# RMS norms of a transformer kernel: the squares of the last feature blocks go to TensorE as further operands of the sum over partitions

## The chip, the cores and the metric

The kernel runs on one core of one Trainium2 chip. The metric is the device time of one execution in microseconds (us), given as the median of three runs. Five parts of the core matter here: PE (TensorE; its weight loads are listed apart as PEld), DVE (VectorE), ACT (ScalarE), POOL (GpSimd), and the DMA queue that SP (SyncE) issues.

## What is computed

Two blocks, one after the other, on 256 tokens of 1024 features. The first has two attention branches and a mixture of experts; the second has two layers, each with a half feed-forward, a mixing step and another half feed-forward, and it works on a second stream of 256 context tokens beside the first. Between the steps stand RMS norms, and this change is about those:

```python
def _rmsnorm(x, g):
    x32 = x.astype(jnp.float32)
    y = x32 * lax.rsqrt(jnp.mean(x32 * x32, axis=-1, keepdims=True) + EPS)
    return (y * g.astype(jnp.float32)).astype(x.dtype)

def _half_ffn(h, g, shift, scale, gate, w_up, w_down):
    return h + 0.5 * gate * _swiglu(_modulate(_rmsnorm(h, g), shift, scale), w_up, w_down)
```

For one token a norm needs the sum of the squares of its 1024 features.

## The kernel before

The hidden state `h` lies with features on the 128 partitions: eight blocks of 128 features (index `d`, 0 to 7), each with 512 columns, of which 256 are the tokens of stream `v` = 0 and 256 those of stream 1. The sum over a token's features is therefore a sum over eight blocks and then over partitions.

A weight matrix comes by DMA as fp32, is split into a high and a low part (`split_w`, ACT L228 and mostly DVE L237, sometimes POOL L235), and each product is three matmuls, lines L250, L251 and L252. This stream of matmuls is nearly all that PE does. Tiles named `pab` are the first product of a feed-forward, `pd` its second, `pj` an input projection and `po` the output of mixing.

A norm is made of these steps:

- As blocks of `h` are finished (DVE L700, `residual`), ACT squares them: two blocks at a time in `square` (L345), one at a time in `square1` (L356). The squares land in a scratch tile `sq`, and scratch tiles rotate through seven buffers.
- POOL adds the squares to a running sum `sqa` of 128 x 256 (L349 for the first pair; L351 adds the halves of a later pair, and L352 adds that to `sqa`; L357 adds a single block).
- The last pair (`i == last`) or the last block (`d == 7`) is added by DVE in place of POOL. In the output of a feed-forward, blocks 6 and 7 come singly: 6 is added by POOL and 7 by DVE. In mixing and in the first block all four pairs are added as pairs, the last one by DVE with two additions.
- `rstd` (L319) sums over partitions: for each half of 128 tokens one matmul with the squares as its weights and a single column of ones as the moving operand, into the tile `ss`. Then DVE makes `nv` (L325) and the reciprocal root (`rsqrt`, L292 to L303).
- `spread` (L315) turns the result into a row for all partitions (tile `rb`), and `apply` makes the next step's operands `xH` and `xL` from it (DVE L333, ACT L338, DVE L339).

There are twelve such norms in an execution. Seven follow a feed-forward and use `square1`; five use `square` alone: one of the context tokens, one ahead of the experts, two after the mixing of layer 0, and one after the mixing of layer 1. The last of the five is used late: its factor is applied to the product of the next feed-forward and not to its input (`late_norm`, L372). After the last feed-forward, `finish` (L1739) scales `h`, transposes it (`op`, L1749) and writes it out.

The order in which instructions stand on an engine comes from a scheduler that works with its own cost estimates; generators with constants such as `NORM_LAG` say only after how many steps of the main work a norm's parts are recorded. On an engine, instructions run in the order in which they stand.

Of the kernel before, what the change touches and what calls it, by code (L numbers as in the profile page):

```python
# [12 lines left out]
ALU = mybir.AluOpType  # L13
# [5 lines left out]
S = 256  # L19
# [151 lines left out]
class Builder:  # L171
# [147 lines left out]
    def rstd(self, sq):  # L319
        nc = self.nc  # L320
        ss = self.nps("ss")
        for t in range(2):
            nc.tensor.matmul(ss[:, t:t + 1], sq[0][:, t * 128:(t + 1) * 128], self.ones[:, 0:1], start=True, stop=True)
        m = self.small([128, 2], "nv")
        nc.vector.tensor_scalar(m, ss[:, :2], 1.0 / D, EPS, ALU.mult, ALU.add)  # L325
        return self.rsqrt(m, 2, "nr")
# [14 lines left out]
    def square(self, v, i, sq, last=3):  # L341
        nc = self.nc
        t = self.s512("sq")
        hs = self.h[:, 2 * i:2 * i + 2, v * S:(v + 1) * S]
        nc.scalar.activation(t.rearrange("p (j t) -> p j t", j=2), hs, AF.Square)  # L345
        e = nc.vector if i == last else nc.gpsimd
        if not sq:
            sq.append(self.scr.tile([128, S], F32, tag="sqa", name="sqa", bufs=2))
            e.tensor_tensor(sq[0], t[:, :S], t[:, S:], ALU.add)  # L349
        else:  # L350
            e.tensor_tensor(t[:, :S], t[:, :S], t[:, S:], ALU.add)  # L351
            e.tensor_tensor(sq[0], sq[0], t[:, :S], ALU.add)  # L352

    def square1(self, v, j, sq, e):
        t = self.s512("sq")[:, :S]
        self.nc.scalar.activation(t, self.h[:, j, v * S:(v + 1) * S], AF.Square)  # L356
        e.tensor_tensor(sq[0], sq[0], t, ALU.add)  # L357

    def normed(self, l, n, v, sq):
        for _ in range(NORM_LAG[v][0 if n < 2 else 2]):  # L360
# [228 lines left out]
    def ffn(self, l, n, up, dn, vs, side, pace, after):  # L589
        nc = self.nc  # L590
        self.raw_n, self.raws = 0, 7
        half = lambda v: slice(v * S, (v + 1) * S)
        with ExitStack() as st:
# [9 lines left out]
            for pi, nf in enumerate(PARTS):  # L603
# [6 lines left out]
                for c in range(nf // 2):  # L610
# [4 lines left out]
                    for i in range(2):  # L615
# [20 lines left out]
                        for z in range(0, len(todo), 2):  # L636
                            pa, pb = todo[z][1][:, full], todo[z + 1][1][:, full]
                            if late:
                                p = pabs.pop(0)
                                ab = self.small([128, 2], "ab")  # L640
                                s = self.s512("fs").rearrange("p (a t) -> p a t", a=2)
# [4 lines left out]
                                t = self.s512("ft")[:, full]  # L646
                                nc.vector.scalar_tensor_tensor(t, s[:, 1], ab[:, 1:2], s[:, 0], ALU.add, ALU.mult)
                            else:
                                s = self.s512("fs")[:, full]
                                nc.scalar.activation(s, pa, AF.Silu)  # L650
                                t = self.s512("ft")[:, full]
# [9 lines left out]
                if pi < len(PARTS) - 1:  # L661
                    for dc in range(4):
                        v = self.rows(dn, f0 * 128, nf, dc * 256, 256)
                        for i in range(2):
                            w = self.split_w(v[:, :, i * 128:(i + 1) * 128], off_dn)
                            p = self.mm("pd")
                            self.gemm(p[:, full], w, lambda f: hid[f])
                            for v2 in range(N // S):
                                self.residual(p[:, half(v2)], 2 * dc + i, l, n, v2)
                        for _ in range(pace[1] if N == full_n else 1):  # L670
                            next(side, None)
                else:
                    ws = [self.split_w(self.rows(dn, f0 * 128, nf, dc * 256, 256), OFF_256) for dc in range(4)]
                    for v in sorted(vs):
                        sq = []
                        for d in range(KD):
                            cs = slice(d % 2 * 128, d % 2 * 128 + 128)
                            w = [z[:, :, cs] for z in ws[d // 2]]
                            p = self.mm("pd")[:, :S]
                            self.gemm(p, w, lambda f: (hid[f][0][:, half(v)], hid[f][1][:, half(v)]))  # L680
                            self.residual(p, d, l, n, v)
                            next(side, None)
                            self.advance()
                            if d >= 6:
                                self.square1(v, d, sq, nc.vector if d == 7 else nc.gpsimd)
                            elif d % 2:
                                self.square(v, d // 2, sq)
                        for _ in side:
                            pass
                        self.settle()  # L690
                        if after is not None:
                            self.pending = self.normed(*after, v, sq)
                        else:
                            self.sq = sq
# [1107 lines left out]
```

## Time and profile before

| | |
|---|---|
| median of 3 runs | 2226.15 us (2225.15 to 2231.33) |
| the profiled execution | 2228.05 us |
| its span in the trace | 2226.3 us |
| PE busy, share of the span | 2157.4 us, 97% |
| PEld busy | 1779.4 us, 80% |
| DVE busy | 1437.8 us, 65% |
| ACT busy | 816.7 us, 37% |
| POOL busy | 170.9 us, 8% |
| granted TensorE clock, mean | 0.993 |

The profiled execution is 1.75 us longer than its span, and 1.9 us above the median. Matmuls overlap each other and their weight loads, so the duration of one is not its price: the price is the step from one start to the next.

### The profile page before, as it was taken

How to read it: one execution, taken by the hardware profiler on the slowest of the kernel's cores; microseconds unless marked ns; L12 is line 12 of the kernel's file. 1: busy time of each engine (PE TensorE's matmuls, PEld its weight loads, DVE VectorE, ACT ScalarE, POOL GpSimd, SP SyncE). 2: the span in 40 equal slices, each digit the busy share in tenths (PEclk: the TensorE clock that was granted, in tenths of full speed). 3: DMA queues.
4: the chain of work that ended last, by engine and by line, in shares of the span. 5: the costliest groups of instructions: out<-in, count | busy, mean ns of one | idle time of the engine just before them, and what ended most of it. 6: DMA issues, size and time to landing. Idle time of an engine off the chain costs nothing.

```text
span 2226.3 us, 32470 instructions
## 1 busy us (share of the span) xinstructions
PE 2157.4 (97%) x13295; PEld 1779.4 (80%) x13295; DVE 1437.8 (65%) x2520; ACT 816.7 (37%) x1256; POOL 170.9 (8%) x200
## 2 busy tenths in 40 slices
PE   8999999997999999989999999999999999999998
PEld 7789975543688888977888777788878888889998
DVE  5656852321489787766678777638974346877666
ACT  4564431200233322447542222234222223575443
POOL 0100100000000000340120000000000003312000
PEclk9999999999999999999999999999999999999999
DMA  8673869998956654320236555343553222317551
GB/s 259 230 242 129 274 226 353 361 387 350 336 169 212 226 187 151 88 66 29 97 123 200 182 189 181 127 132 112 192 189 100 90 66 73 105 34 246 176 174 48
DMA packets 285461, 395.91 MB, mean 178 GB/s; under 512 B 18156, under 2 KB 220540, under 8 KB 285180
## 3 DMA queue, kind: packets, MB, share of 16 engines
q1 hardware_dynamic: 284288, 392.33, 52.2%
q8 instruction: 106, 1.74, 0.3%
q0 software_dynamic: 576, 1.18, 0.2%
q14 instruction: 47, 0.39, 0.0%
q10 hardware_dynamic: 444, 0.27, 0.0%
HBM read 392.71 MB, written 1.05 MB: 177 GB/s over the span
## 4 chain that ended last, share of the span: by engine, by line
PE 68%; DVE 5%; ACT 1%; POOL 1%; issue 1%; DMA 0%; ACTq 0%; POOLq 0%; DVEq 0%
PE pab L250 12%; PE pab L251 12%; PE pab L252 12%; PE pd L250 6%; PE pd L251 6%; PE pd L252 6%; PE pj L250 1%; PE pj L252 1%; PE pj L251 1%; PE egu L1164 1%; PE aT L1654 1%; PE as L1625 1%; DVE w L237 1%; PE ada_ps L533 1%; PE ao L1671 1%; DVE xL L339 1%
## 5 line engine op out<-in xcount | busy, mean ns | idle before, releaser
L228 ACT ACTIVATE w<-raw 128x1024 fp32r<-128x1024 f32 (+2 forms) x432 | 425.8, 991 | 667.4 <-PE pd L252 240.5
L237 DVE TENSOR_TENSOR w<-raw,w 128x1024 fp32r<-128x1024 f32 (+2 forms) x422 | 481.5, 1151 | 185.8 <-ACT w L228 184.0
L251 PE MATMUL pab<-xL,w 128*128 128x512 f32 (+2 forms) x1600 | 545.7, 342 | 2.6 <-DVE xL L339 1.6
L250 PE MATMUL pab<-xH,w 128*128 128x512 f32 (+2 forms) x1600 | 546.0, 342 | 0.1
L252 PE MATMUL pab<-xH,w 128*128 128x512 f32 (+2 forms) x1600 | 544.1, 340 | 0.0
L250 PEld LDWEIGHTS pab<-xH,w 128*128 128x128 f32 x1600 | 301.4, 189 | 48.9 <-issue 8.2
L251 PEld LDWEIGHTS pab<-xL,w 128*128 128x128 f32 x1600 | 301.8, 189 | 42.3 <-issue 4.1
L252 PEld LDWEIGHTS pab<-xH,w 128*128 128x128 f32 x1600 | 301.7, 189 | 37.9 <-issue 4.1
L551 DVE SCALAR_TENSOR_TENSOR acc<-raw,sT,acc 128x512 f32<-128x512 f32 x420 | 285.0, 748 | 0.0
L250 PE MATMUL pd<-hH,w 128*128 128x512 f32 (+1 forms) x800 | 265.4, 334 | 0.5 <-ACT hH L241 0.3
L251 PE MATMUL pd<-hL,w 128*128 128x512 f32 (+1 forms) x800 | 265.0, 332 | 0.0
L252 PE MATMUL pd<-hH,w 128*128 128x512 f32 (+1 forms) x800 | 264.5, 332 | 0.0
L250 PE MATMUL pj<-xH,w 128*128 128x256 f32 (+1 forms) x816 | 247.8, 305 | 12.0 <-DVE qra L1553 5.2
L251 PE MATMUL pj<-xL,w 128*128 128x256 f32 (+1 forms) x816 | 242.8, 298 | 1.5 <-DVE xL L339 0.5
L252 PE MATMUL pj<-xH,w 128*128 128x256 f32 (+1 forms) x816 | 241.9, 297 | 0.5 <-DVE w L237 0.5
L250 PEld LDWEIGHTS pj<-xH,w 128*128 128x128 f32 x816 | 154.7, 190 | 26.5 <-DVE qra L1553 6.0
L700 DVE SCALAR_TENSOR_TENSOR h<-pd,gmod,h 128x256 f32<-128x256 f32 x224 | 101.0, 480 | 101.3 <-PE pd L252 101.2
L250 PEld LDWEIGHTS pd<-hH,w 128*128 128x128 f32 x800 | 149.8, 188 | 20.4 <-ACT fs L650 3.4
L252 PEld LDWEIGHTS pd<-hH,w 128*128 128x128 f32 x800 | 149.9, 188 | 16.7 <-issue 1.7
L251 PEld LDWEIGHTS pd<-hL,w 128*128 128x128 f32 x800 | 150.8, 188 | 15.5 <-DVE hL L242 0.3
L251 PEld LDWEIGHTS pj<-xL,w 128*128 128x128 f32 x816 | 155.1, 190 | 7.2 <-DVE xL L339 2.2
L252 PEld LDWEIGHTS pj<-xH,w 128*128 128x128 f32 x816 | 154.8, 190 | 5.5 <-DVE w L237 0.8
(388 smaller groups left out, 2456.3 us busy)
## 6 DMA issues: line engine op xcount, KB each, us to landing
raw<-ffn_up SPq DMA_DIRECT2D x94, 1024.0 KB, 5.3
raw<-w_ada SPq DMA_DIRECT2D x72, 1024.0 KB, 5.3
raw<-ffn_down SPq DMA_DIRECT2D x52, 768.0 KB, 4.7
raw<-w_in SPq DMA_DIRECT2D x32, 1024.0 KB, 5.5
raw<-w_exp_gate SPq DMA_DIRECT2D x32, 1024.0 KB, 9.7
raw<-w_exp_up SPq DMA_DIRECT2D x32, 1024.0 KB, 10.0
raw<-w_exp_down SPq DMA_DIRECT2D x32, 1024.0 KB, 8.8
raw<-w_gate SPq DMA_DIRECT2D x8, 1024.0 KB, 5.7
```

Of the source, the lines that this page charges most:

```text
L228: self.nc.scalar.activation(wh, v, AF.Copy)
L237: self.nc.vector.tensor_tensor(wl, v, wh.bitcast(F32), ALU.subtract)
L250: mm(o, wH[:, k, :], aH, start=(first and k == 0), stop=False)
L251: mm(o, wH[:, k, :], aL, start=False, stop=False)
L252: mm(o, wL[:, k, :], aH, start=False, stop=(last and k == n - 1))
L339: nc.vector.scalar_tensor_tensor(lo, t, B(j), hi.bitcast(F32), ALU.add, ALU.subtract)
L533: mm(ps[g * 32:(g + 1) * 32, :], self.unit[:, 31 - r:63 - r], acc[v], start=(u < 2), stop=(u > 3))
L551: ins = V.scalar_tensor_tensor(acc[v], w[:, g, :], s, acc[v], ALU.mult, ALU.add)
L700: self.nc.vector.scalar_tensor_tensor(hs, p, self.gmod[:, l, n, d, v:v + 1], hs, ALU.mult, ALU.add)
L1164: mm(pr[a * 64:a * 64 + 64, m, :], xg[p // 2][:, q * 2 + kk, es[a] % 4 * 64:es[a] % 4 * 64 + 64], w[:, a, kk * 512:(kk + 1) * 512], start= ...
L1625: mm(o[:, c], qs, x[i][:, c], start=(i == 0 and not (near and c.start == 0)), stop=(i == 1))
L1654: nc.tensor.transpose(T[:, j * 128:(j + 1) * 128], e[:, a, j * 128:(j + 1) * 128], self.ident)
```

## The change

`square` and `square1` no longer add the last squares to the running sum. They put the tiles of squares into a list behind it, and `rstd` runs one matmul for each operand of the list, all accumulating into the same column of `ss`. In every norm the list then has three operands: `sqa` with six blocks, and the last two blocks.

```diff
@@ rstd
         for t in range(2):
-            nc.tensor.matmul(ss[:, t:t + 1], sq[0][:, t * 128:(t + 1) * 128], self.ones[:, 0:1], start=True, stop=True)
+            for i, s in enumerate(sq):
+                nc.tensor.matmul(ss[:, t:t + 1], s[:, t * 128:(t + 1) * 128], self.ones[:, 0:1],
+                                 start=(i == 0), stop=(i == len(sq) - 1))
@@ square
-        e = nc.vector if i == last else nc.gpsimd
-        if not sq:
+        e = nc.gpsimd
+        if i == last:
+            sq.extend((t[:, :S], t[:, S:]))
+        elif not sq:
             sq.append(self.scr.tile([128, S], F32, tag="sqa", name="sqa", bufs=2))
             e.tensor_tensor(sq[0], t[:, :S], t[:, S:], ALU.add)
         else:
             e.tensor_tensor(t[:, :S], t[:, :S], t[:, S:], ALU.add)
             e.tensor_tensor(sq[0], sq[0], t[:, :S], ALU.add)
 
-    def square1(self, v, j, sq, e):
+    def square1(self, v, j, sq):
         t = self.s512("sq")[:, :S]
         self.nc.scalar.activation(t, self.h[:, j, v * S:(v + 1) * S], AF.Square)
-        e.tensor_tensor(sq[0], sq[0], t, ALU.add)
+        sq.append(t)
@@ ffn
-                                self.square1(v, d, sq, nc.vector if d == 7 else nc.gpsimd)
+                                self.square1(v, d, sq)
```

The instructions also change places, since the scheduler orders them anew. On PE, at the end of the first feed-forward of layer 0 (first of its two norms), the difference reads (- before, + now):

```order
 L251 MATMUL pd<-hL,w 128x256
 L252 MATMUL pd<-hH,w 128x256
-L323 MATMUL ss<-sqc,sqa 128x1 x2
+L324 MATMUL ss<-sqc,sqa 128x1
+L324 MATMUL ss<-sqc,sq 128x1 x2
+L324 MATMUL ss<-sqc,sqa 128x1
+L324 MATMUL ss<-sqc,sq 128x1 x2
 L250 MATMUL pd<-hH,w 128x256
 L251 MATMUL pd<-hL,w 128x256
```

Two matmuls became six at the same place in the stream. So it is in five of the norms: the first one, and the first norm of each of the four pairs.

On PE in the first part of the last feed-forward (the late norm), two pieces. Before, the two matmuls stood here:

```order
L252 MATMUL pab<-xH,w 128x258
L323 MATMUL ss<-sqc,sqa 128x1 x2
L250 MATMUL pab<-xH,w 128x258
L251 MATMUL pab<-xL,w 128x258
L252 MATMUL pab<-xH,w 128x258
```

Now the matmul on `sqa` stands 34 matmuls further ahead, between products that were there before, and the other five stand 20 matmuls ahead of the old place:

```order
 L250 MATMUL pab<-xH,w 128x258 x2
 L251 MATMUL pab<-xL,w 128x258
+L324 MATMUL ss<-sqc,sqa 128x1
 L252 MATMUL pab<-xH,w 128x258
 L250 MATMUL pab<-xH,w 128x258
```

The second norm of each of the four pairs is moved ahead in the same way, by smaller distances.

On PE at the end of the program, the matmuls on squares now stand before and after nine of the sixteen transposes of the output:

```order
 L251 MATMUL pd<-hL,w 128x256
 L252 MATMUL pd<-hH,w 128x256
-L323 MATMUL ss<-sqc,sqa 128x1 x2
-L1749 MATMUL op<-sqc,h 128x128 x16
-L1798 UNCONDITIONAL_BRANCH
+L324 MATMUL ss<-sqc,sqa 128x1
+L324 MATMUL ss<-sqc,sq 128x1
+L1753 MATMUL op<-sqc,h 128x128 x9
+L324 MATMUL ss<-sqc,sq 128x1
+L324 MATMUL ss<-sqc,sqa 128x1
+L324 MATMUL ss<-sqc,sq 128x1 x2
+L1753 MATMUL op<-sqc,h 128x128 x7
```

At that place one addition of POOL and one of DVE (L357) are gone. Around the experts' start the order of the first products and of the routing is changed in several rows, on PE, DVE and ACT.

## Rows read from the trace of the kernel before

**Rows 1.** The page: busy time of the engines (share of the span, instructions).

```profile
PE 2157.4 (97%) x13295; PEld 1779.4 (80%) x13295; DVE 1437.8 (65%) x2520; ACT 816.7 (37%) x1256; POOL 170.9 (8%) x200
```

**Rows 2.** Instructions by tile, `sqa`: count, duration in ns (min/median/max), first and last start.

```profile
L323 PE MATMUL ss<-sqc,sqa x48: 164/250/271, 259.2 to 2218.0; 128*128 128x1 f32 x48
...
L357 POOL TENSOR_TENSOR sqa<-sqa,sq x7: 730/744/823, 907.0 to 2215.9; 128x256 f32<-128x256 f32 x7
L357 DVE TENSOR_TENSOR sqa<-sqa,sq x7: 414/426/427, 908.0 to 2217.2; 128x256 f32<-128x256 f32 x7
L352 DVE TENSOR_TENSOR sqa<-sqa,sq x5: 419/421/426, 246.2 to 2027.7; 128x256 f32<-128x256 f32 x5
```

**Rows 3.** Timeline at the first norm: start, duration, engine, [idle before <- releaser].

```profile
259.07 0.53 PEld L323 LDWEIGHTS ss<-sqc,sqa 128*128 128x128 f32 x4
...
259.51 0.19 PEld L250 LDWEIGHTS pj<-xH,w 128*128 128x128 f32 x1
```

**Rows 4.** Timeline at the norm that follows the experts, matmuls of two columns.

```profile
594.59 0.98 PEld L1213 LDWEIGHTS sums<-fin,sq 128*128 128x128 f32 x8
...
595.49 0.19 PEld L251 LDWEIGHTS pab<-xL,w 128*128 128x128 f32 x1
```

**Rows 5.** Timeline at the last norm.

```profile
2216.64 0.42 ACT L356 ACTIVATE sq<-h 128x256 f32<-128x256 f32 x1 [0.87 <-DVE h L700]
2217.16 0.43 DVE L357 TENSOR_TENSOR sqa<-sqa,sq 128x256 f32<-128x256 f32 x1 [0.61 <-ACT sq L356]
...
2217.64 0.61 PE L323 MATMUL ss<-sqc,sqa 128*128 128x1 f32 x4 [3.97 <-DVE sqa L357]
...
2218.28 0.16 DVE L325 TENSOR_SCALAR nv<-ss 128x2 f32<-128x2 f32 x1 [0.43 <-PE ss L323]
```

**Rows 6.** Timeline at the norm ahead of the experts.

```profile
281.54 0.61 PE L323 MATMUL ss<-sqc,sqa 128*128 128x1 f32 x4 [0.81 <-DVE sqa L352]
```

**Rows 7.** The waits of PE, whole span: us in total, times, longest.

```profile
PE rb L315 <- DVE nr_y L303: 1.9, 4, 0.6
...
PE pab L251 <- DVE xL L339: 1.6, 5, 0.6
...
PE pab L251 <- DVE xL L1496: 0.7, 3, 0.3
...
PE pj L251 <- DVE xL L339: 0.5, 2, 0.3
```

**Rows 8.** Timeline: transposes of the second norms after the first feed-forward, both layers.

```profile
929.22 0.45 PE L315 MATMUL rb<-sqc,nr_y 128*128 128x128 f32 x2 [0.50 <-DVE nr_y L303]
...
1892.07 0.45 PE L315 MATMUL rb<-sqc,nr_y 128*128 128x128 f32 x2 [0.56 <-DVE nr_y L303]
```

**Rows 9.** Timeline at the late norm.

```profile
2024.59 0.28 PE L252 MATMUL pab<-xH,w 128*128 128x258 f32 x1
...
2024.64 1.76 DVE L237 TENSOR_TENSOR w<-raw,w 128x1024 fp32r<-128x1024 f32 x1
...
2025.39 1.60 POOL L352 TENSOR_TENSOR sqa<-sqa,sq 128x256 f32<-128x256 f32 x1
...
2027.33 0.39 PE L251 MATMUL pab<-xL,w 128*128 128x258 f32 x1 [0.18 <-DVE xL L1496]
```

**Rows 10.** Timeline at two second norms: after mixing, and after a feed-forward.

```profile
1135.17 0.81 POOL L352 TENSOR_TENSOR sqa<-sqa,sq 128x256 f32<-128x256 f32 x1
1135.21 0.28 PE L250 MATMUL pab<-xH,w 128*128 128x256 f32 x1
...
1510.28 0.80 POOL L352 TENSOR_TENSOR sqa<-sqa,sq 128x256 f32<-128x256 f32 x1
...
1510.88 0.28 PE L250 MATMUL pab<-xH,w 128*128 128x256 f32 x1
```

**Rows 11.** Stretches with idle PE: length, busy times of engines, granted clock, DMA share, GB/s.

```profile
397.50:401.00 3.50, 2.62 (x25) 2.29 (x26) 1.79 (x3) 1.79 (x4) 0.00 (x0) 0.79 1.02 408
...
520.00:527.00 7.00, 1.64 (x8) 1.67 (x9) 0.76 (x2) 0.00 (x0) 0.00 (x0) 0.67 1.02 399
```

**Rows 12.** The waits of SP's DMA queue from 255 to 300 us.

```profile
SPq L216 <- DVE rt_1x L1258: 15.0, 1, 15.0
```

## The prediction

> **What bounds the kernel now.** I read the busy times first. PE is busy for 97% of the span, and no other engine comes near [rows 1]; work added to PE is paid unless it falls into one of PE's few idle gaps. Then I took the tile of the running sum, to count what goes and what grows [rows 2]; the timeline at the norms, for what one more matmul costs in a full stream [rows 3, 4]; PE's waits, for where a shorter norm could give something back [rows 5 to 8]; and, with the order of instructions shown above, the places to which matmuls moved, to see whether their operands are there by then [rows 9, 10].
>
> **What is removed.** DVE loses 7 + 5 additions into the sum [rows 2] and 5 that add the halves of a pair, 17 of about 0.42 us, 7 us in all. POOL loses 7 of 0.74 us [rows 2], 5 us. Neither engine is the bound [rows 1]. These additions cost something only where PE waits for them, and PE does that twice: 3.97 us at the end, most of it for the last products' results and not for the addition, and 0.81 us ahead of the experts [rows 5, 6].
>
> **What is added.** 12 norms x 2 halves x 2 operands are 48 matmuls. The 24 of before are 48 records [rows 2], since an fp32 matmul is carried out as two; so 96 records more, 8 for each norm. The price of a record is the step between weight loads, because each of these matmuls brings a full 128 x 128 load for one column of work. Four records at the first norm take 259.51 - 259.07 = 0.44 us until the next product's load, 0.110 each [rows 3]. Eight records of a similar kind take 595.49 - 594.59 = 0.90 us, 0.1125 each [rows 4]. I take 0.111: 0.89 us for each norm, **+10.7 us** for twelve.
>
> A rule speaks about this price. The Trainium skill's page "TensorE: Matmul & The Clock Gate", section "Back-to-back issue gap", gives matmuls of 1 to 64 columns an issue floor of about 25 ns and says that this leaves weight loads out. By that floor the term would be, as an estimate, 96 x 0.025 = 2.4 us, and the whole sum would be some 8 us lower. The two groups of rows just read speak for the load.
>
> **What of it is covered.** At the end of the program PE sits idle for 3.97 us [rows 5]; the matmuls on `sqa` and block 6 fit there, and those on block 7 can begin when ACT ends at 2217.06, where the old pair waited until 2217.64. They are more, so `nv` comes at much the same time, perhaps 0.1 us sooner; nine transposes are done earlier. I take -0.9 for the cover of this norm's records and -0.2 for the tail. Ahead of the experts the 0.81 us gap [rows 6] now holds products that stood behind it: -0.8. Left: 10.7 - 0.9 - 0.2 - 0.8 = **+8.8 us**.
>
> **What waits give back.** PE waits for DVE's norm chain in four places at `rb`, 1.9 us, and ten times at `xL`, 1.6 + 0.7 + 0.5 us [rows 7]: 4.7 us at most. A wait behind the first norm of a pair starts from that norm's own matmuls, so it shifts with them and stays. A wait behind the second norm hangs on DVE still working on the first one's `apply`, while PE arrives 0.89 us later; it goes. Those are 0.50 and 0.56 us [rows 8], and I count the two waits at `pj` with them, 0.5: **-1.5 us**, between 0 and -4.7.
>
> **What new waits come.** Instructions on PE run in order, so a matmul on `sqa` that stands earlier than POOL's last addition holds up all products behind it. At the late norm it now stands where PE is at 2024.59; POOL's last addition starts at 2025.39 and takes 1.60, to 2026.99 [rows 9]. Neither the squares nor POOL's work ahead of it is changed, so PE should stand 2.4 us there, less the 0.2 it waited at 2027.33 anyway: +2.2. After mixing in layer 0 it stands at 1135.21 and `sqa` is ready at 1135.98: +0.8. After the second feed-forward of layer 0, 1510.88 against 1511.08: +0.2 [rows 10]. At the second norms after the first feed-forward of both layers POOL is done before PE arrives. Together **+3.2 us**. POOL's end is the roughest of these figures, and 1.60 is twice the usual duration, beside a split of DVE that also took long, 1.76 [rows 9]; with the usual 0.80 the three would be 2.4. The bounds are 0 (the squares come earlier, now that DVE has less to do) and 4.
>
> DVE's `nv` of the late norm now stands ahead of a weight split and would hold it up; I cost that at nothing, because weights are split several products ahead. The three scratch tiles that now wait for the matmul in place of an addition rotate among seven; nothing too. If that cover is gone, DVE or ACT waits for a buffer, at most one step of 0.9 us for each norm.
>
> **The part that the trace of before can't price.** Around the experts' start the order of routing, splits and products changes. SP waited 15.0 us there for one instruction of the routing before it could load expert weights [rows 12], and in the experts the DMA engines are full (share 1.02, PE busy 1.64 of 7 us in one stretch) [rows 11]. An instruction of DVE now stands ahead of it that waits for a split. Earlier by the two additions gone is -0.85 us, later by one split of 1.2 us is +1.2; some products move too. I take 0, with -3 and +3 as ends, for three such displacements.
>
> **Sum.** 10.7 - 0.9 - 0.2 - 0.8 - 1.5 + 3.2 = **+10.5 us**. The profiled execution took 2228.05, so 2238.6; it was 1.9 above the median, and on the median's scale the forecast is 2226.15 + 10.5 = **2236.6 us**, 0.47% slower. About 0.3%, 6.7 us, is what a measurement of this kernel can tell from no change.
>
> **Rivals.**
>
> 1. *The shorter norm pays for itself (no change).* Each norm's chain loses an addition of DVE, 0.43 us or 0.85, and often one of POOL. If that, and not PE's arrival, decides the ten `xL` and four `rb` waits, they all go, 4.7 us, and the new waits don't come: 10.7 - 1.9 - 4.7 = +4.1, 2230.3. It decides from the point where DVE's chain starts before the matmuls and not behind them. For it: PE waits on exactly these tiles. Against it: in five norms the six matmuls stand where two stood, so `nv` comes 0.44 to 0.89 us later there, not sooner. Chance 0.13.
>
> 2. *The loads slip into free time (no change).* PEld is busy for 80% [rows 1], so 447 us are free. If the scheduler's spreading lets the added loads run under neighbouring products, the records cost next to nothing, and 3.2 - 1.5 - 0.2 = +1.5 is left: 2227.7. The issue floor on the page of the Trainium skill named above is this case. Against it: in both groups of rows each load took its full step. This is also the case in which the change does not do what it says. Chance 0.07.
>
> 3. *The stall slows the clock (slower still).* In 397.5 to 401 us, with PE idle for 0.9, the granted clock was 0.79; in 520 to 527, 0.67 [rows 11]. If the 2.4 us stall at the late norm does this, the cost is 3.5 x 0.21 = 0.7 to 7 x 0.33 = 2.3 us: 2237.3 to 2238.9. The Trainium skill, same page, section "What's actually happening", says that the slow clock is the default and that activity releases it; the trace agrees with these two stretches. Chance 0.10.
>
> 4. *The experts start later.* Routing delayed by a split, with transfers full behind it: up to +3, 2239.6. Chance 0.12.
>
> **How the numbers follow.** The forecast has 0.58, and rivals 1 to 4 have 0.13, 0.07, 0.10 and 0.12. Slower by over 0.3%: the forecast and rivals 3 and 4, 0.80, less 0.03 for a forecast with no stalls and a good start of the experts: 0.77. Rivals 1 and 2 and most of that are no change: 0.20. Faster, 0.03, needs rival 2 and the experts' start at -3 and more. The range goes from rival 1's 2230.3, a little lower for a better start of the experts, 2230, to +3 for the experts and +2.3 for the clock on the forecast, 2242.
>
> **What would show it.** The group on `ss` should have 144 records, and at the first feed-forward's end 12 of them should take about 1.33 us. DVE should lose 17 additions and POOL 7. PE's waits should have a new line, `ss` waiting for POOL's `sqa`, about 3 us in three places, the longest 2.4 near 2025 to 2035; the line with 3.97 should be shorter and the `rb` line near 0.9. I am wrong if the step of the added records is well under 0.1 us, if the new line is missing, or if the span of the experts moves by more than 3 us.

## The result, and the profile after

The changed kernel takes 2236.78 us (median of 16 runs, 2232.03 to 2248.94), the kernel before 2226.55 us (16 runs, 2221.64 to 2234.71). The ratio is 1.0051, with a 95% interval of 1.004 to 1.0063: 0.5% slower, some 11 us. The forecast was 2236.6, 10.5 us more. The number was met; three of its terms were not, and their errors had opposite signs.

The profiled execution of the changed kernel took 2240.55 us. The line of the page that answers to [rows 1]:

```profile
PE 2173.3 (97%) x13391; PEld 1796.6 (80%) x13391; DVE 1431.7 (64%) x2503; ACT 816.5 (36%) x1256; POOL 162.5 (7%) x193
```

PE has 96 records more, DVE 17 instructions fewer and POOL 7 fewer. PE is busy 16 us longer. By tile, the matmuls on `ss` (count, duration in ns as min/median/max, first and last start):

```profile
L324 PE MATMUL ss<-sqc,sq x96: 164/250/353, 258.9 to 2230.4; 128*128 128x1 f32 x96
...
L324 PE MATMUL ss<-sqc,sqa x48: 164/250/373, 258.7 to 2229.5; 128*128 128x1 f32 x48
```

That is 144 records. What they cost in a full stream is read at the first feed-forward's end, in the timeline of PEld (start, duration), from the first load of the group to the next product's load:

```profile
913.21 0.30 PEld L324 LDWEIGHTS ss<-sqc,sqa 128*128 128x128 f32 x2
...
913.43 0.53 PEld L324 LDWEIGHTS ss<-sqc,sq 128*128 128x128 f32 x4
...
913.87 0.30 PEld L324 LDWEIGHTS ss<-sqc,sqa 128*128 128x128 f32 x2
...
914.10 0.53 PEld L324 LDWEIGHTS ss<-sqc,sq 128*128 128x128 f32 x4
...
914.54 0.19 PEld L250 LDWEIGHTS pd<-hH,w 128*128 128x128 f32 x1
```

Twelve records take 914.54 - 913.21 = 1.33 us, which is the figure forecast. The matmuls themselves (timeline of PE), now and then before, at the same place:

```profile
913.32 0.28 PE L324 MATMUL ss<-sqc,sqa 128*128 128x1 f32 x2
...
914.57 0.36 PE L250 MATMUL pd<-hH,w 128*128 128x256 f32 x1
```

```profile
909.50 0.50 PE L323 MATMUL ss<-sqc,sqa 128*128 128x1 f32 x4
909.86 0.36 PE L250 MATMUL pd<-hH,w 128*128 128x256 f32 x1
```

Between the first matmul of the group and the next product it is 1.255 us for twelve records, and 0.361 for the four of before (by the unrounded starts). So an added record costs (1.255 - 0.361) / 8 = 0.112 us.

The waits of PE (us in total, times, longest), against [rows 7]:

```profile
PE ss L324 <- POOL sqa L356: 4.0, 3, 2.3
...
PE pab L251 <- DVE xL L341: 1.1, 3, 0.6
...
PE ss L324 <- ACT sq L360: 0.7, 1, 0.7
PE pj L251 <- DVE xL L341: 0.6, 3, 0.3
...
PE pab L251 <- DVE xL L1500: 0.5, 2, 0.3
```

The new line for `sqa` on POOL is there, with a longest wait of 2.3. The line for `rb`, 1.9 us before, is gone altogether, and the longest wait at the end of the program, 3.97 us [rows 5], is gone too.

At the late norm, POOL and PE (timeline), and then busy times, granted clock and DMA share by stretch:

```profile
2032.73 1.59 POOL L356 TENSOR_TENSOR sqa<-sqa,sq 128x256 f32<-128x256 f32 x1
...
2034.37 0.59 PE L324 MATMUL ss<-sqc,sqa 128*128 128x1 f32 x2 [2.26 <-POOL sqa L356]
```

```profile
2028.00:2032.00 4.00, 3.35 (x23) 2.63 (x21) 4.00 (x9) 3.27 (x7) 3.92 (x6) 1.00 0.37 113
2032.00:2036.00 4.00, 1.74 (x8) 1.63 (x8) 2.60 (x3) 0.65 (x2) 2.24 (x2) 0.57 1.03 341
2036.00:2040.00 4.00, 4.00 (x22) 4.00 (x20) 0.00 (x0) 0.00 (x0) 0.00 (x0) 0.50 1.10 355
2040.00:2044.00 4.00, 4.00 (x24) 4.00 (x25) 2.65 (x15) 1.06 (x1) 0.00 (x0) 0.65 1.10 349
2044.00:2050.00 6.00, 6.00 (x52) 6.00 (x52) 4.93 (x13) 4.72 (x5) 0.00 (x0) 1.00 0.47 149
```

PE stands 2.26 us on `sqa`, as forecast, and is busy for 1.74 of 4 us. Behind that the granted clock is 0.50, the lower of its two levels (1.2 GHz), until past 2040, although PE is busy without a gap from 2036 on: it runs 22 records in 4 us there, where the kernel with the sum last (below) ran 35 at 1.00. The Trainium skill's page "TensorE: Matmul & The Clock Gate", section "What's actually happening", has the low clock as the default, which activity lifts; the trace agrees in that the clock fell with the stall.

**Where the time went, stretch by stretch.** All kernels here run the same 13247 records of products and transposes beside those on `ss`. So the start of the n-th such record can be compared between two traces, and the difference of two of them is what a stretch gained or lost. The table gives that difference in us against the first profile of the kernel before (+ is longer); stretches are named by their times in it. The last column is explained where the kernel before is run again. Each row is one execution; the rows below the second are the experiments of the next section.

| execution | experts 280-589 | 2nd norm 917-960 | 2 norms 1109-1147 | no norm 1147-1479 | 2 norms 1479-1521 | no norm 1521-1848 | 2 norms 1848-1967 | late norm 2021-2061 | no norm 2061-2162 |
|---|---|---|---|---|---|---|---|---|---|
| changed | +2.34 | +0.47 | +1.11 | 0.00 | +0.33 | 0.00 | +1.45 | +6.56 | -2.85 |
| changed, again | -1.13 | +0.42 | +1.10 | -0.04 | +0.33 | 0.00 | +1.97 | +5.86 | -2.85 |
| before, again | +0.79 | -0.01 | +0.01 | -0.03 | +0.02 | 0.00 | +0.01 | -0.01 | -2.85 |
| late norm later | -0.18 | +0.42 | +1.09 | -0.04 | +0.37 | -0.01 | +1.28 | +1.82 | -2.84 |
| late norm undone | +3.82 | +0.39 | +1.08 | -0.04 | +0.37 | -0.01 | +0.91 | -0.43 | -1.43 |
| late norm alone | +0.06 | -0.03 | +0.01 | -0.03 | +0.02 | 0.00 | +0.60 | +3.63 | -2.86 |
| `square1` alone | +2.82 | +0.68 | +0.03 | -0.04 | +0.33 | 0.00 | +0.55 | -0.67 | -2.88 |
| four early norms alone | -2.45 | -0.30 | +1.09 | -0.05 | -0.02 | -0.01 | +0.41 | -1.05 | -1.44 |
| sum last | +1.02 | +0.72 | +0.97 | -0.01 | +0.40 | -0.01 | +0.55 | +0.89 | -2.87 |
| operands doubled | +1.28 | +1.59 | +4.29 | 0.00 | +1.97 | 0.00 | +6.30 | +9.36 | -2.85 |
| fp32r, tiles moved | +0.54 | +0.21 | +0.05 | +5.31 | -0.07 | +5.62 | +0.56 | +0.07 | -1.60 |
| before, fp32r, tiles moved | +1.73 | -0.49 | -0.21 | +5.73 | +0.45 | +5.62 | +0.37 | -0.24 | -1.10 |
| fp32r, nothing moved | -0.28 | +1.68 | +0.11 | -0.04 | -0.25 | -0.01 | -0.07 | +0.26 | -2.85 |

Three things are seen at once. The late norm is the one large loss, 6.56 us where the forecast had 3.1. The seven other norms in these stretches, whose 8 records cost 0.89 us each, lost less than that: 0.47 for one, 1.11, 0.33 and 1.45 for pairs (1.97 for the last pair in the second profile; the clock has a part there, see below). And the experts differ by -2.45 to +3.82 between executions, whether the change touches that place or not.

### The profile page after: what moved, and what is told of

It reads as the page before. It is cut to its first block, busy times and chain, and to the rows that moved or that the text cites. A ratio compares the mean times of both kernels' runs of the same rounds, so it can differ in the third digit from the quotient of the medians.

```text
span 2238.8 us, 32622 instructions
## 1 busy us (share of the span) xinstructions
PE 2173.3 (97%) x13391; PEld 1796.6 (80%) x13391; DVE 1431.7 (64%) x2503; ACT 816.5 (36%) x1256; POOL 162.5 (7%) x193
## 3 DMA queue, kind: packets, MB, share of 16 engines
HBM read 392.71 MB, written 1.05 MB: 176 GB/s over the span
## 4 chain that ended last, share of the span: by engine, by line
PE 69%; DVE 3%; POOL 2%; ACT 1%; issue 1%; DVEq 0%; POOLq 0%; ACTq 0%
PE pab L250 12%; PE pab L252 12%; PE pab L251 12%; PE pd L250 6%; PE pd L251 6%; PE pd L252 6%; PE pj L250 2%; PE pj L251 2%; PE pj L252 2%; PE egu L1168 1%; PE aT L1658 1%; PE as L1629 1%; PE ao L1675 1%; PE po L250 1%; PE ada_ps L537 1%; PE po L252 1%
```

## The experiments

Theory: the stall at the late norm and the low clock behind it are the larger part of the loss, and the added records are mostly paid back by waits of PE that go. One rival: the records are the loss, 0.89 us for each norm. The other: the experts start later.

### The changed kernel again

> The changed kernel once more, for the spread of its parts from one execution to the next. Theory (the late norm's stall and the half clock behind it are the larger part of the loss): median 2236 to 2238, and in the profile the stall of PE on sqa near 2032 is again 2.2 to 2.4 us with about 8 us at half clock behind it. Rival (the added records and the experts' start are the loss, the stall was an accident of one execution): the stall is under 1.5 us or the clock stays full, at the same median. Between 290 and 600 us the first execution lost 3.4 us against before; if that is the change it comes back within 1 us, if it is the transfers' chance it moves by more.

2236.54 us (6 runs), ratio 1.0042 (1.0028 to 1.0057). With the first comparison, that is 9 to 11 us over before. The stall is 2.27 us again and the low clock follows again. The experts' stretch came out at -1.13 where it had been +2.34: chance, not the change.

### The late norm's matmuls later

```diff
-LATE_LAG = (2, 2)
+LATE_LAG = (5, 2)
```

> The changed kernel with one constant larger (the late norm is recorded three steps later): of the twelve norms only the late one moves, to 51 matmuls behind where its first one stood; its six matmuls on squares stay together. Theory (stall and half clock): the stall of 2.3 us on sqa and the half clock are gone, the records stay, so 2.3 + 3.4 = 5.7 us less than the changed kernel, about 2231. Rival (records): no change against the changed kernel, 2236 to 2237. Rival (only the stall counts, the half clock would come anyway): 2.3 us less, 2234.5.

Ratio 1.0031 (1.0019 to 1.0043), 2235.89 us: by the ratios 2.4 to 4.5 us less than the two comparisons of the changed kernel, not 5.7, and by the medians less than 1. The trace says why it is less: the wait on `sqa` and the low clock are gone from the stretch (granted clock 1.00 throughout 2024 to 2040), but the factor now comes late, and PE waits 1.05 us for it at `rb` (stretch, then timeline). The stretch is at +1.82 in place of 6.56 and 5.86. The direction is the theory's, the size a miss.

```profile
2028.00:2032.00 4.00, 3.84 (x33) 3.64 (x32) 2.18 (x3) 1.06 (x1) 1.60 (x1) 1.00 1.07 362
```

```profile
2039.13 0.45 PE L315 MATMUL rb<-sqc,nr_y 128*128 128x128 f32 x2 [1.05 <-DVE nr_y L303]
```

### The late norm undone, and the late norm alone

```diff
-                        self.square(v, d // 2, sq, 2 if v else 3)
+                        self.square(v, d // 2, sq, 2 if v else 3, full)
```

The new argument says whether the last pair goes to PE; `full` is true in layer 0 alone. The second kernel passes `not full`, and leaves `square1` and the other calls of `square` as they were before.

> The changed kernel with the late norm's last pair added by DVE as before, so that its two matmuls stand in their old place; the eleven other norms stay changed. Theory (stall and half clock): 6.6 us less than the changed kernel, about 2230.2. Rival (records, 0.89 us each norm): 0.9 us less, 2235.9. My forecast had 3.1 us for this norm: 2233.7.

> The kernel before with only the late norm changed; its six matmuls on squares stand where they do in the changed kernel. Theory (stall and half clock): 6.6 us over before, about 2233, with 8 us at half clock behind a stall of 2.3 us. Rival (records): 0.9 us over before, 2227.4. My forecast: 3.1 us, 2229.6. The step between matmuls from 2064 to 2170 us, 0.118 and 0.121 before and 0.113 and 0.118 in the changed kernel, may give 2.8 us back here too, if it is the stall that sets it.

Undone: ratio 1.0017 (1.0005 to 1.0028), 2233.2 us. Against the changed kernel's 1.0042 and 1.0051 that is 5.6 to 7.6 us less (by the medians 3.3 and 3.6). Alone: ratio 1.0027 (1.0016 to 1.0038), 6.0 us over before. Both are nearer to the theory's 6.6 than to the 0.9 of its records. The stall is the same with this one norm changed, and the clock falls with it, for a shorter time (timeline; then the stretches):

```profile
2028.43 0.38 PE L324 MATMUL ss<-sqc,sqa 128*128 128x1 f32 x2 [2.27 <-POOL sqa L356]
```

```profile
2024.00:2028.00 4.00, 1.65 (x10) 1.07 (x8) 4.00 (x6) 2.41 (x4) 3.84 (x5) 1.00 0.88 265
2028.00:2032.00 4.00, 3.56 (x19) 3.57 (x20) 0.67 (x1) 0.00 (x0) 0.38 (x1) 0.63 1.09 365
2032.00:2036.00 4.00, 4.00 (x33) 4.00 (x33) 2.35 (x15) 1.06 (x1) 0.00 (x0) 0.94 1.10 348
```

### The kernel before again

> The kernel before once more, one look. In the profile of before the matmuls from 2063 to 2160 us went at steps of 0.1178 (pd) and 0.121 us (pab), in five profiles of changed kernels mostly at 0.1133 and 0.1178, 2.85 us less over this stretch in four of them, even where nothing was changed ahead of 2021 us. If the slow step belongs to the kernel before, it is there again; if it was the chance of one execution, this profile shows 0.1133 and 0.1178, and the stretch takes 2.8 us less.

2225.88 us, one run. The faster step from one matmul to the next (the 0.1133 and 0.1178 us above) is there, in the kernel before: the 2.85 us of the last column were the chance of its first profile. The two executions of before, in stretches of 30 us of `pab` (PE records in brackets, granted clock third from the end), first the one of the tables ahead, then this one:

```profile
2080.00:2110.00 30.00, 30.00 (x250) 30.00 (x249) 20.93 (x41) 13.61 (x20) 0.00 (x0) 1.00 0.54 177
```

```profile
2078.00:2108.00 30.00, 30.00 (x257) 30.00 (x257) 20.71 (x41) 14.67 (x21) 0.00 (x0) 1.00 0.58 187
```

The same products at the same clock, 250 records against 257.

### Parts of the change

`square1` alone: the five calls of `square` keep their last pair on DVE. The four early norms: `square1` and the late norm as before.

> Only square1 changed (the seven norms that follow a feed-forward), the other five norms as before. Theory (what a norm costs is 8 records less the waits that its shorter chain takes away; stalls and clock decide elsewhere): by the stretches of the two profiles of the changed kernel about 3 us over before, 2230. Rival (records at full price, 0.89 each, less the cover at the end): 5.3 us, 2232. My forecast had 4.3.

> Only four of the five norms that use square alone changed: context, ahead of the experts, and the two after mixing of layer 0. Theory: by the stretches of the changed kernel 1.1 us for the two after mixing, some 0.4 for the context, nothing ahead of the experts: 1.5 us over before, 2228.5. My forecast had 0.89 + 0.1 + 1.78 + 0.8 - 0.25 = 3.3 us, 2230.3. Rival (the experts start later): 3 us more than that, and in the profile the experts' stretch is 3 us longer than before. Together with the runs of the late norm alone and of square1 alone the three should add up to the changed kernel's 10.3 us.

Ratios 1.0003 (0.999 to 1.0015) and 1.0003 (0.9987 to 1.0018): neither can be told from no change. For `square1` this is against the records at full price (5.3 us; the interval ends at 3.3) and against my 4.3. The stretches repeat those of the full change to 0.1 us where the same norms are changed and the clock is full: +0.33 at 1479, +1.09 at 1109. The sum 0.7 + 0.7 + 6.0 = 7.4 us falls short of the changed kernel's 9 to 11, within intervals of some 3 us on each part. The experts were 2.45 us shorter in the profile of the kernel that changes their start, and 2.82 longer in the one that doesn't: nothing speaks for a later start.

### The running sum as last operand

```diff
+        sq = sq[1:] + sq[:1]
         for t in range(2):
             for i, s in enumerate(sq):
```

> The changed kernel with the running sum as the last operand of each group in place of the first. Nothing is added or removed; on PE the early matmuls on sqa go back to the others: 6 matmuls at the norm ahead of the experts, 12 after mixing in layer 0, 14 at the late norm. Theory (stalls on sqa and the half clock behind them): the stall of 0.8 us is gone, that of 2.3 falls to 0.6, and if the shorter one leaves the clock full, 3.4 us more: 2.5 to 5.9 us less than the changed kernel, 2231 to 2234. Rival (records): no change, 2236.5.

Ratio 1.0014 (1.0 to 1.0028), 2231.56 us: by the ratios 6 to 8 us less than the changed kernel (by the medians 5), though no record is saved. The late norm's stretch is at +0.89, the price of its 8 records. Its wait and its clock:

```profile
2031.25 0.38 PE L325 MATMUL ss<-sqc,sqa 128*128 128x1 f32 x2 [0.24 <-POOL sqa L357]
```

```profile
2028.00:2032.00 4.00, 3.65 (x30) 3.57 (x30) 3.48 (x5) 1.21 (x3) 3.12 (x3) 1.00 1.02 337
2032.00:2036.00 4.00, 4.00 (x35) 4.00 (x35) 3.02 (x16) 1.06 (x1) 0.00 (x0) 1.00 1.08 358
```

A wait of 0.24 us left the clock at 1.00; the wait of 2.26 did not. After mixing in layer 0, though, where the same edit took away a stall of 0.8 us, the stretch went only from 1.10 to 0.97. PE's steps there show why: the waits for `xL` of the kernel before (steps of 0.32 and 0.41 us from 1136.05 on) had gone into the stall, and came back without it (0.31 and 0.41 from 1138.53 on).

### Twice the added operands

```diff
+        sq = sq + sq[1:]
         for t in range(2):
             for i, s in enumerate(sq):
```

> The changed kernel with the two last operands of every norm given to PE twice, at the same places: 48 matmuls, 96 records more than the changed kernel (the sum then counts the last two feature blocks double, so the output is another). A block of 12 records in a full stream took 1.255 us in the changed kernel where 4 took 0.361: 0.112 a record. Theory A (the first 96 records have used up PE's waits for the norm's chain): the next 96 cost 0.112 each less what the end of the program covers, 9 to 10 us over the changed kernel, 2246. Theory B (waits still take up two thirds in the pairs of norms): 4 us, 2240.5.

Ratio 1.0129 (1.0107 to 1.0151), 2258.03 us: by the ratios 17 to 19 us over the changed kernel (by the medians 21), more than either theory. In the pair at 1479, where the clock stayed full, the second 16 records cost 1.97 - 0.33 = 1.64 us of 16 x 0.112 = 1.79; the first 16 had cost 0.33. That is theory A, for this pair: the first helping was paid with waits, the second in full. What both theories missed is the clock. More one-column matmuls stand together, and at such places the granted clock is low for longer, or where it had been full in the changed kernel:

```profile
1900.00:1908.00 8.00, 8.00 (x46) 8.00 (x47) 7.69 (x24) 1.42 (x4) 7.98 (x12) 0.62 1.07 203
2044.00:2060.00 16.00, 13.73 (x69) 13.63 (x69) 5.77 (x20) 1.79 (x4) 2.23 (x2) 0.57 0.97 316
```

Over the whole run the clock is 0.982 here, 0.987 and 0.989 in the two profiles of the changed kernel.

### One record for each matmul

Squares and ones as fp32r, so that a matmul is one record of two columns:

```diff
-                nc.tensor.matmul(ss[:, t:t + 1], s[:, t * 128:(t + 1) * 128], self.ones[:, 0:1],
+                nc.tensor.matmul(ss[:, 2 * t:2 * t + 2], s[:, t * 128:(t + 1) * 128], self.ones_r,
...
         self.xH = C.tile([128, KD, T2], F32R, name="xH")
+        self.ones_r = C.tile([128, 2], F32R, name="ones_r")
+        nc.scalar.activation(self.ones_r, self.ones[:, :2], AF.Copy)
```

with three operands (sum last), and in the kernel before with its one operand:

> The kernel with the running sum as last operand, and now with the squares and the ones kept as fp32r, so that each matmul on squares is one record of two columns in place of two of one: 72 records in place of 144, at the same places. If a record's price is paid, 72 x 0.112 = 8 us less than the kernel with the sum last (2231.6, 3.1 over before): 2223.5, 3 to 5 under before. If the pairs of norms are bound by the chain behind the matmuls, and records in them cost a third, 3 us less: 2228.5, as before. Against the kernel before it has 24 records more and 17 + 7 additions fewer.

> The kernel before with the running sum and the ones kept as fp32r: 24 records of two columns in place of 48, additions and places as before. If a record's price is paid, 24 x 0.112 = 2.7 us less than before, of which the end of the program and the norm ahead of the experts cover some 0.5: 2224 to 2224.5. If the chain behind the matmuls binds, it gains a little more, since every norm's factor comes 0.22 us sooner: 12 x 0.22 = 2.7 again, 5 us at most. Compared with the kernel with fp32r and three operands this says whether giving the last squares to PE is worth its place once a record is cheap.

Both missed by over 20 us, 1.0098 (1.008 to 1.0116) and 1.0097 (1.008 to 1.0114). The table shows where: +5.3 to +5.7 us in each of the stretches of 332 and 327 us that hold no norm; most of the rest lies ahead of 280 us (5.5 and 5.0 us) and from 589 to 917 us (3.6 and 4.2), outside the table. The new tile of two columns stood between `xH` and `xL`, ahead of all later tiles. So it was put into columns of a filler tile that is otherwise unused:

```diff
-        C.tile([128, LEAD], F32, name="lead")
+        lead = C.tile([128, LEAD], F32, name="lead")
+        self.ones_r = lead[:, :2].bitcast(F32R)
+        nc.scalar.activation(self.ones_r, self.ones[:, :2], AF.Copy)
```

> The two runs with fp32r had a constant of two columns placed between the two halves of the split activations, and lost 5.3 to 5.7 us in each of the two stretches of 332 and 327 us that hold no norm at all (1147 to 1479 and 1521 to 1848 us): every tile behind it had moved. Here the constant lies in columns of a filler tile that was there before, so nothing moves; else it is the kernel with fp32r, three operands and the sum last. If the move was the loss, both stretches are back within 0.1 us of before, and the time is 2223.5 if a record's price is paid (72 records of 0.112 less than the kernel with the sum last), 2228.5 if the pairs of norms are bound by the chain. If fp32r itself slows the products, the stretches stay 5 us longer and the time is about 2249.

Both stretches are back at -0.04 and -0.01, so the move was the loss, and not fp32r. The time is 2230.68 us, ratio 1.002 (1.0004 to 1.0036): neither of the two values, and no better than the kernel with the sum last. In the three pairs the stretches went from 0.97, 0.40 and 0.55 to 0.11, -0.25 and -0.07: 2.1 us for 36 records fewer, half of 36 x 0.112 = 4.0. So even here half a record's price is paid by waits. In the profile the gain was lost between 589 and 917 us, which took 4.9 us longer than before. The granted clock was lower there: 0.78 over the first 31 us of that stretch and 0.92 over its last 21, against 0.92 and 1.00 over such stretches before. The profile with the late norm undone shows the same, 0.78 and 0.91, and took 5.9 us longer from 589 to 917 us. What lowered the clock there was not settled. No version beat the kernel before.

## Why the prediction came out right, and where its steps did not

- **The records.** Forecast 0.111 us each and 10.7 in all; measured 0.112. The load sets the price, as [rows 3, 4] had it. The issue floor of about 25 ns from the Trainium skill (page "TensorE: Matmul & The Clock Gate", section "Back-to-back issue gap") leaves loads out, as it says itself, and was not the price here.
- **The cover: right ahead of the experts, wrong at the end.** The wait of 0.81 us ahead of the experts is gone. At the end the forecast was 0.89 - 0.9 - 0.2 = -0.2, with `nv` perhaps 0.1 us sooner. From 2162 us to the start of the last transpose the two profiles did lose only 0.17 and -0.14 us. But the time runs on until the output is written, and all profiles here have 8.0 us from `nv` to their end; `nv` came 1.44 and 1.12 us later than in the first profile of before, 1.05 and 0.73 later than in the second. Only four of the twelve records went into the idle time. The other eight stand behind the nine transposes, and from 2229.03 to 2230.59 they took 1.56 us, at a granted clock of 0.50 (timeline):

```profile
2227.67 0.42 ACT L360 ACTIVATE sq<-h 128x256 f32<-128x256 f32 x1 [0.87 <-DVE h L704]
...
2229.03 0.42 PE L324 MATMUL ss<-sqc,sq 128*128 128x1 f32 x2
2229.31 0.56 PE L324 MATMUL ss<-sqc,sqa 128*128 128x1 f32 x2
2229.74 0.99 PE L324 MATMUL ss<-sqc,sq 128*128 128x1 f32 x4
2230.59 1.73 PE L1753 MATMUL op<-sqc,h 128*128 128x128 f32 x7
...
2230.77 0.16 DVE L327 TENSOR_SCALAR nv<-ss 128x2 f32<-128x2 f32 x1 [2.30 <-PE ss L324]
```

  Here `nv` starts 2.68 us after the last squares are done; before it was 1.22 [rows 5]. Profiles with this end have 1.5 to 2.7 us, those with the end of before 1.2 to 1.6. How much of it is the clock was not separated.
- **What waits give back: the step "-1.5 us, between 0 and -4.7" was mis-sized.** By the stretches, the second norm at 917 gave back 0.89 - 0.47 = 0.42; the pair at 1109, with its new stall of 0.8, 1.78 + 0.8 - 1.11 = 1.47; the pair at 1479, with its new wait of 0.2, 1.78 + 0.2 - 0.33 = 1.65, the one at 1848 1.78 - 0.55 = 1.23 (the value with a full clock, from `square1` alone). Together 4.8 us, which I had held to be the bound for all waits. Two things were overlooked. First, I held that a wait behind a norm's own matmuls "shifts with them and stays"; the `rb` line went from 1.9 us to nothing. Second, the bound itself was too low, because a wait's idle time is counted from the modelled end of the matmul ahead, and that end lies far behind the next start in a full stream. At a norm of before (timeline of PE, one matmul's step and the wait that the view gives):

```profile
1517.04 0.28 PE L250 MATMUL pab<-xH,w 128*128 128x256 f32 x1
1517.62 0.39 PE L251 MATMUL pab<-xL,w 128*128 128x256 f32 x1 [0.29 <-DVE xL L339]
1517.84 0.28 PE L252 MATMUL pab<-xH,w 128*128 128x256 f32 x1
```

  The step is 0.58 us and the next 0.22, where a full stream has 0.12: 0.56 us are lost, and the wait reads 0.29. In the changed kernel the same three stand like this, with no wait shown:

```profile
1523.31 0.28 PE L250 MATMUL pab<-xH,w 128*128 128x256 f32 x1
1523.51 0.39 PE L251 MATMUL pab<-xL,w 128*128 128x256 f32 x1
1523.73 0.28 PE L252 MATMUL pab<-xH,w 128*128 128x256 f32 x1
```

- **The new waits.** Forecast 2.2, 0.8 and 0.2. At the late norm 2.26, less the 0.2 of before; at 1140 the step onto `sqa` is 0.92 us in place of 0.12, at 1517 0.36. Right in place and size, though the one at 1140 cost little, since other waits went into it. At the second norms after the first feed-forwards, where the forecast had POOL done before PE arrives, the step is 0.37 and 0.38 as well (at 925 and 1890 us): two waits of 0.25 us that it did not have. The 4.8 us above are what is left after these two.
- **The clock: forecast 0, with rival 3 beside it at a chance of 0.10 and a price of 0.7 to 2.3 us.** Rival 3 came true at the late norm, at a higher price. The late stretch less its 8 records and its stall is 6.56 - 0.89 - 2.06 = 3.6 us in the first profile, 2.9 in the second and 0.7 with the late norm alone. My rows for its price were short idle stretches [rows 11]; here the low clock lasted over products that PE ran without a gap. In the pair at 1848 the clock had a part too: it was 0.97 over the stretch in both profiles, and they lost 1.45 and 1.97 us where `square1` alone lost 0.55 at 1.00, so 0.9 and 1.4 us more. Some of that may be chance: the kernels with the late norm alone and with the four early norms alone leave that pair as it was, and lost 0.60 and 0.41 there at 0.99.
- **The experts.** Forecast 0, within 3; from -2.45 to +3.82 without regard to the change. Within the bounds, but it is noise and not a term.

With the sizes measured in the two profiles (means of both where they differ) the sum is 9.8 for the records of eleven norms, +1.3 at the end, -0.8 ahead of the experts, -4.8 and +3.1 for waits that went and came, and +3.2 and +1.2 for the clock at the late norm and at 1848: 13.0. The two profiles, less the experts and the last column, are 13.0 and 12.0 us longer than the first of before (spans of 2238.8 and 2234.3 against 2226.3). The many runs give 9 to 11. So the forecast's 10.5 was partly luck: waits gave back 3.3 us more than it had, and the clock took 4.4 and the end 1.5 that it did not have. Of the prediction's rivals, the first was right in mechanism for the pairs of norms and the third for the late norm; the second is refuted by the step of 0.112, and nothing in the experts speaks for the fourth.

Left open: the 2 us by which the profiles' sum is above the runs; the sum of the parts, 7.4, against the whole; and why the kernel with fp32r and nothing moved was not faster than the one with the sum last.

## What to carry to other kernels

Before moving work onto the bound engine, look where the operand comes from that its first instruction needs: here the late norm, with one matmul 34 products further ahead, cost 6 us, the eleven other norms together some 4 to 6, and changing the order of three operands took 5 to 8 us back. Price a wait by the step from start to start, not by the idle time beside it; and where a stall of some 2 us is forecast on TensorE, allow for a stretch of low clock behind it (here 0.7 to 3.6 us; the stall of 0.8 us at 1140 brought none). Follow the end of the program to the last write, not to TensorE's last matmul. Compare more than one execution of each kernel before a difference of 3 us in a stretch is called an effect.

## What the runs showed of the hardware

- A stream of the same products at granted clock 1.00 runs at one of two steps for 100 us on end: 0.1178 or 0.1133 us for `pd` (256 columns), 0.121 or 0.1178 for `pab` (258 columns). Which one it is changed between executions of one kernel; over 2061 to 2162 us it is worth 2.85. In two profiles it changed in the middle of that stretch (-1.43 and -1.44).
- A constant of eight bytes a partition, placed between the two halves of the split activations, made two stretches of products of 512 columns 1.6 to 1.7% longer (5.3 to 5.7 of 332 and 327 us), with nothing else changed there. In the filler tile it cost nothing.
- The granted clock can be low where the page shows no idle PE: in the kernel with operands doubled it was 0.62 from 1900 to 1908 us, with PE busy for 8.00 us and a group of 16 one-column records among its work.
